# The factor on the probabilities as a constant 67th row of the score product, and a 66-column transposition of the maxima

## The chip, the core and the metric

The kernel runs on one core of one Trainium2 chip. The metric is the device time of one execution in microseconds (us), as a median over runs. Five engines work side by side, each with a queue of its own: TensorE (PE; its weight loads are shown apart as PEld), VectorE (DVE), ScalarE (ACT), GpSimd (POOL) and SyncE (SP), which here issues the DMA transfers.

## What is computed

One encoder layer is applied to 2048 and to 512 tokens of width 1024: normalisation, one projection, attention beside a two-way gated linear attention, an output projection, an embedding gate and a last normalisation. The change lies in the attention. There are 8 query heads and 2 key heads of width 64:

```python
s = jnp.einsum('bkgqd,btkd->bkgqt', q_blk, k).astype(jnp.float32) * scale
p = jax.nn.softmax(s, axis=-1)
return jnp.einsum('bkgqt,btkd->bkgqd', p.astype(v.dtype), v)
```

## The kernel before

Stage 1 projects and rotates, stage 2 builds the linear attention, stage 3 is the attention with the gates, stage 4 the output. Stage 3 works through 40 items: a block of 512 queries of one head. The first four blocks have 2048 keys (16 key tiles of 128), the fifth has 512 (4 tiles), so there are 32 x 16 + 8 x 4 = 544 key tiles in all.

Queries and keys are split into a high and a low half of 16 bits. Two products of 512 columns (L861, L862) put the transposed scores of one key tile into PSUM (`pss`): `qa` and `ka` hold 128 rows, `qb` and `kb` hold 64 rows of q's high half and k's low half, and two rows more. In these rows `kb` has the constant 4096 (L747, written by POOL) and `qb` has minus the query's maximum over 4096, as a 16-bit value and its rest. So the score comes out with the maximum already taken off. ScalarE then makes the probability `p` (L863): exp(qk_scale * pss + ln 256), where the scale `qk_scale` and the bias `lnp` are both a column of one value for each partition. It rounds `p` to 16 bits (`phi`, L870), two key tiles at a time; VectorE takes the rest (`plo`, L872); TensorE multiplies both by the values (`po`, L842 and L850) and by ones (`pz`, L846). L842 and L846 use 32 columns of weights at a time, at four places of the array, the other products 128.

The maxima are computed some heads' tiles ahead (function `maxima`): products `px` (L807), a reduction of each by VectorE (`mx`, L813), one over the tiles (L817), and two instructions that write `mt`, 128 x 4 blocks x 2 (L821, L822). Four products (L825) with the 2 columns of a block of `mt` as weights and the identity as the moving operand, 128 columns wide, turn it into two rows of 512 in a `px` buffer of PSUM. ScalarE copies the two rows to partitions 64 and 65 of `qb` (L826).

The order on each queue is set as follows. `stage3` walks over the items; in `head`, after each Exp, `pull` takes steps from generators: the maxima of later items (`mg`, with counts in `steps`), the rest of stage 2 (`fin`), the gates (`gt`, L773), the sums and the stores. `tc.issue_after(e.ins)` puts what a step issues on ScalarE behind that Exp. Buffers are reused in turn: 4 for `qa` and for `qb`, 3 for `mt`, `p` and the small tiles, 2 and then 3 of PSUM for `pss`, 2 for `px`. `load_q` issues the two loads of an item from SP (L755, L756) when its maxima begin.

Of the kernel before, what the change touches and what calls it, by code (L numbers as in the profile page):

```python
# [9 lines left out]
F32 = mybir.dt.float32  # L10
F32R = mybir.dt.float32r
F16 = mybir.dt.float16
BF16 = mybir.dt.bfloat16
U32 = mybir.dt.uint32
AF = mybir.ActivationFunctionType
ALU = mybir.AluOpType
# [4 lines left out]
P = 128  # L21
# [3 lines left out]
P_SCALE = 256.0  # L25
V_LIMIT = 1024.0
QK_SCALE = 1024.0
M_SCALE = 4096.0
# [27 lines left out]
class Net:  # L56
    def __init__(self, tc, d, ctx):
        self.tc, self.nc, self.d = tc, tc.nc, d
        nc = self.nc
        nc.scalar.preload_act_table_set("natural_log_exp_and_others")  # L60
        self.cp = ctx.enter_context(tc.tile_pool(name="cp", bufs=1))
        self.sm = ctx.enter_context(tc.tile_pool(name="sm", bufs=3))
        self.ident = self.cp.tile([P, P], F32, name="ident")
        make_identity(nc, self.ident)
        self.identh = self.cp.tile([P, P], F16, name="identh")
        nc.vector.tensor_copy(self.identh, self.ident)
        self.lnp = self.cp.tile([P, 1], F32, name="lnp")
        nc.vector.memset(self.lnp, math.log(P_SCALE))
        self.qk_scale = self.cp.tile([P, 1], F32, name="qk_scale")
        self.mhalf = self.cp.tile([P, 1], F32, name="mhalf")  # L70
        nc.vector.memset(self.mhalf, -0.5)
        self.half = self.cp.tile([P, 1], F32, name="half")
        nc.vector.memset(self.half, 0.5)
        self.one = self.cp.tile([P, 1], F32, name="one")
        nc.vector.memset(self.one, 1.0)
        self.plen = self.cp.tile([P, 8], F32, name="plen")
        self.vinv = self.cp.tile([P, 2], F32, name="vinv")

        self.wdiv = self.cp.tile([P, 3], F32, name="wdiv")
# [38 lines left out]
def stage1(net, s, gw):  # L118
    nc, tc, d = net.nc, net.tc, net.d
    with ExitStack() as ctx:  # L120
# [223 lines left out]
        nc.scalar.activation(qa, qn, AF.Abs)  # L344
        big = net.sm.tile([P, 2], F32, name="big")
        nc.vector.tensor_reduce(big, qa, axis=AX.X, op=ALU.max)
        nc.vector.tensor_scalar(big, big, 1e-18, None, ALU.max)
        inv = net.sm.tile([P, 2], F32, name="inv")
        nc.vector.reciprocal(inv, big)
        for w in range(2):  # L350
# [363 lines left out]
def stage3(net, s, fin=iter(()), top=None, tail=None):  # L714
    nc, tc, d = net.nc, net.tc, net.d
    with ExitStack() as ctx:
# [3 lines left out]
        cp = pool("s3c", 1)  # L720
# [3 lines left out]
        qp = pool("s3q", 4)  # L724
# [10 lines left out]
        ones = cp.tile([P, 32], F16, name="ones")  # L735
        nc.vector.memset(ones, 1.0)

        def load_k(c):
            kp = kl[c]
            ka = kp.tile([P, 2, 512], F16, name="ka")  # L740
            kb = kp.tile([P, 2, 512], F16, name="kb")
            v = kp.tile([P, 4, 2, P], F16, name="v")
            src = s["kt"][c].rearrange("l (k d) t -> l d k t", k=2)
            for j in range(2):
                nc.sync.dma_start(out=ka[j * 64:(j + 1) * 64], in_=src[0])
            nc.sync.dma_start(out=kb[0:64], in_=src[1])
            nc.gpsimd.memset(kb[64:66], M_SCALE)  # L747
            nc.sync.dma_start(out=v, in_=s["vs"][c].rearrange("t p k e -> p t k e"))
            return ka, kb, v

        def load_q(c, h):
            src = s["qt"][c][:, h // 2, (h % 2) * 64:(h % 2) * 64 + 64]
            qa = qp.tile([P, 512], F16, name="qa")
            qb = qp.tile([P, 512], F16, name="qb3")
            nc.sync.dma_start(out=qa, in_=src)  # L755
            nc.sync.dma_start(out=qb[0:64], in_=src[0])  # L756
            return qa, qb
# [43 lines left out]
        def maxima(idx, c, h, q):  # L801
            ks = keys(c)
            n = len(ks)
            mx = net.sm.tile([P, 4, n], F32, name=f"mx{n}")
            def product(ti, b):
                ps = ps_x.tile([P, 512], F32, name="px", tag="px")
                nc.tensor.matmul(ps, lhsT=q[0][:, b * P:(b + 1) * P], rhs=ks[ti][0][:, h // 4],  # L807
                                 start=True, stop=True)
                return ps

            for b in range(4):
                for i in range(n):
                    nc.vector.tensor_reduce(mx[:, b, i:i + 1], product(i, b), axis=AX.X, op=ALU.max)  # L813
                    yield
            if n > 1:
                m = net.sm.tile([P, 4], F32, name="m")
                nc.vector.tensor_reduce(m, mx, axis=AX.X, op=ALU.max)  # L817
            else:
                m = mx[:, :, 0]
            mt = net.sm.tile([P, 4, 2], F16, name="mt")  # L820
            nc.vector.tensor_scalar(mt[:, :, 0], m, -1.0 / M_SCALE, None, ALU.mult)  # L821
            nc.vector.scalar_tensor_tensor(mt[:, :, 1], m, -1.0 / M_SCALE, mt[:, :, 0], ALU.mult, ALU.subtract)  # L822
            ps = ps_n_tile()
            for b in range(4):
                nc.tensor.matmul(ps[0:2, b * P:(b + 1) * P], lhsT=mt[:, b], rhs=net.identh, start=True, stop=True)  # L825
            nc.scalar.copy(q[1][64:66], ps[0:2])  # L826

        def head(ks, h, q, ou, pull, last):
            kv = h // 4
# [24 lines left out]
            for t in range(0, n, 2):  # L854
                p = pp.tile([P, 2, 512], F32, name="p", bufs=3)
                for i in range(2):
                    ka, kb = ks[t // 4][:2]
                    cs = slice((t % 4 + i) * P, (t % 4 + i + 1) * P)
                    ps = ps_s[0].tile([P, 512], F32, name="pss")
                    ps_s.append(ps_s.pop(0))  # L860
                    nc.tensor.matmul(ps, lhsT=ka[:, kv, cs], rhs=q[0], start=True, stop=False)  # L861
                    nc.tensor.matmul(ps, lhsT=kb[0:66, kv, cs], rhs=q[1][0:66], start=False, stop=True)  # L862
                    e = nc.scalar.activation(p[:, i], ps, AF.Exp, bias=net.lnp, scale=net.qk_scale)  # L863
                    with tc.issue_after(e.ins):
                        pull(t + i, n)
                hi = pp.tile([P, 2, 512], F16, name="phi", bufs=4)
                if last and t % 8 == 6:
                    nc.vector.tensor_copy(hi, p)
                else:
                    nc.scalar.copy(hi, p)  # L870
                lo = pp.tile([P, 2, 512], F16, name="plo", bufs=4)
                nc.vector.tensor_tensor(lo, p, hi, ALU.subtract)  # L872
                pend.append((t, hi, lo))
                if len(pend) == 3:
                    pv([pend.pop(0) for _ in range(2)])
# [41 lines left out]
        kset, gs, qs = {}, {}, {}  # L917
# [8 lines left out]

        def all_maxima():
            for i, (c, h) in enumerate(items):
                qs[i] = load_q(c, h)
                yield from maxima(i, c, h, qs[i])  # L930
                yield

# [316 lines left out]
```

## Time and profile before

| | us |
|---|---|
| median of 3 runs (2069.65 to 2073.27) | 2069.95 |
| the profiled execution, its own time | 2074.57 |
| its span, first to last instruction | 2072.9 |
| granted TensorE clock over the span | 0.981 of 2.4 GHz |

The page of the profile gives for each engine its busy time, then the span in 40 slices, the DMA queues, the chain of work that ended last, and the costliest groups of instructions. A group's row reads: line, engine, operation, output <- inputs, shapes, count | busy us, mean ns of one | idle time of the engine before it, and who ended it. Matmuls are pipelined, so the start of one to the start of the next is what it costs, not its duration.

### The profile page before, as it was taken

The page shows a single profiled execution, that of the slowest core. Times are in us where ns is not written, and L with a number is a line of the kernel's source. Part 1 is how long each engine was busy: PE and PEld are TensorE (multiplying, and loading weights), DVE is VectorE, ACT ScalarE, POOL GpSimd, SP SyncE. Part 2 cuts the span into 40 slices and gives each one's busy share as a digit, 9 for nine tenths or more (in the row PEclk, how much of TensorE's full clock was granted, in tenths as well). Part 3 has the DMA queues.
Part 4 walks back from the last instruction along what each step waited for, and adds up shares of the span by engine and source line. Part 5 has one row for each costly group of instructions (what it writes and reads, how often), then busy time and mean ns, then how long its engine had stood idle before and what let it go on. Part 6 is the DMA issues. An engine that isn't in the chain of part 4 may idle for free.

```text
span 2072.9 us, 29975 instructions
## 1 busy us (share of the span) xinstructions
PE 1963.8 (95%) x11096; PEld 1224.5 (59%) x11096; DVE 1318.6 (64%) x2272; ACT 1220.7 (59%) x2136; POOL 350.1 (17%) x293
## 2 busy tenths in 40 slices
PE   8999998999879999999999999999978999999998
PEld 6888886555654433433333343343346888888886
DVE  7557755666668889889889988988863222222223
ACT  6645443555548889889889888878863222222222
POOL 2444441000331001011011100101011111111111
PEclk9999999999989999999999999999989999999999
DMA  7745945454666113322223322312235222222220
GB/s 236 223 116 132 225 105 140 119 160 146 208 207 213 61 62 121 95 88 84 82 89 108 111 69 71 110 53 68 83 110 153 86 87 87 87 87 87 82 67 33
DMA packets 264226, 235.79 MB, mean 114 GB/s; under 512 B 107312, under 2 KB 199312, under 8 KB 264080
## 3 DMA queue, kind: packets, MB, share of 16 engines
q1 hardware_dynamic: 263936, 233.36, 37.8%
q8 instruction: 87, 1.43, 0.3%
q14 instruction: 59, 0.48, 0.1%
q0 software_dynamic: 144, 0.52, 0.1%
HBM read 157.46 MB, written 76.37 MB: 113 GB/s over the span
## 4 chain that ended last, share of the span: by engine, by line
PE 69%; DVE 12%; ACT 9%; DMA 5%; issue 3%; POOL 1%; SPq 0%; DVEq 0%; POOLq 0%; ACTq 0%
PE pm L114 38%; PE pg L773 6%; PE po L850 4%; ACT p L863 4%; DVE plo L872 4%; PE px L807 4%; DVE mx L813 3%; PE pss L862 3%; PE pss L861 3%; ACT phi L870 3%; PE pp L114 3%; PE po L842 2%; PE pz L846 2%; DMA scr_ga<-a 1%; DMA qa<-scr_qt 1%
## 5 line engine op out<-in xcount | busy, mean ns | idle before, releaser
L863 ACT ACTIVATE p<-pss,lnp,qk_scale 128x512 f32<-128x512 f32 x544 | 408.0, 781 | 94.6 <-PE pss L862 90.8
L813 DVE TENSOR_REDUCE mx<-px 128x1 f32<-128x512 f32 x544 | 358.8, 683 | 74.2 <-PE px L807 71.7
L872 DVE TENSOR_TENSOR plo<-p,phi 128x1024 f16<-128x1024 f32 x272 | 344.4, 1266 | 37.4 <-ACT phi L870 34.2
L870 ACT CAST phi<-p 128x1024 f16<-128x1024 f32 x270 | 282.9, 1048 | 4.5
L773 PE MATMUL pg<-xt,wg 128*128 128x512 f16 x960 | 277.3, 378 | 0.5
L807 PE MATMUL px<-ka,qa 128*128 128x512 f16 x544 | 199.8, 382 | 20.0 <-DVE mx L813 11.7
L861 PE MATMUL pss<-qa,ka 128*128 128x512 f16 x544 | 206.8, 381 | 10.1 <-ACT p L863 9.3
L862 PE MATMUL pss<-qb,kb 66*128 66x512 f16 x544 | 208.1, 383 | 0.0
L773 PEld LDWEIGHTS <-wg 128*128 128x128 f16 x960 | 92.8, 97 | 119.2 <-issue 10.1
L1182 DVE SCALAR_TENSOR_TENSOR th<-th,pp 128x512 f32<-128x512 f32 (+1 forms) x41 | 27.7, 675 | 190.6 <-ACT th L1181 190.6
L850 PE MATMUL po<-phi,v 128*128 128x512 f16 x544 | 142.2, 384 | 0.0
L1135 ACT CAST hT<-pt 128x512 fp32r<-128x512 f32 x40 | 23.5, 587 | 166.9 <-PE pt L1134 166.9
L114 PE MATMUL pm<-xt,whl 128*128 128x512 f16 x480 | 108.5, 386 | 2.4 <-ACT l L494 2.4
L114 PE MATMUL pm<-wq_h,xt 128*128 128x512 f32 x320 | 104.2, 406 | 4.6 <-ACT xt L239 4.1
L114 PE MATMUL pm<-wo1h,mx 128*128 128x512 f32 x320 | 102.7, 403 | 5.3 <-ACT wo1h L1083 5.3
L1181 ACT ACTIVATE th<-pm,rh 128x512 f32<-128x512 f32 (+1 forms) x41 | 27.8, 679 | 134.7 <-PE pm L114 134.7
L903 POOL TENSOR_TENSOR ou<-ou,rs 128x512 f32<-128x512 f32 x20 | 32.8, 1639 | 435.3 <-DMA rs<-scr_rc 367.6
L114 PE MATMUL pm<-wpg0h,hT 128*128 128x512 f32 x320 | 101.8, 398 | 4.4 <-ACT hT L1135 4.2
L114 PE MATMUL pm<-wo0h,mx 128*128 128x512 f32 x320 | 101.0, 396 | 0.0
L862 PEld LDWEIGHTS <-kb 66*128 66x128 f16 x544 | 53.0, 97 | 79.9 <-issue 22.8
L114 PE MATMUL pm<-wpg1h,hT 128*128 128x512 f32 (+1 forms) x336 | 99.6, 379 | 0.0
L114 PE MATMUL pm<-wl_h,xt 128*128 128x512 f32 x320 | 99.6, 392 | 0.0
(267 smaller groups left out, 3785.0 us busy)
## 6 DMA issues: line engine op xcount, KB each, us to landing
wg<-scr_wg SPq DMA_DIRECT2D x40, 512.0 KB
scr_mx<-hl SPq DMA_DIRECT2D x40, 512.0 KB
mx<-scr_mx SPq DMA_DIRECT2D x20, 1024.0 KB
x<-x_prompt SPq DMA_DIRECT2D x27, 512.0 KB
scr_xt<-xh SPq DMA_DIRECT2D x20, 512.0 KB
xt<-scr_xt SPq DMA_DIRECT2D x20, 512.0 KB
xt<-scr_xt SPq DMA_DIRECT2D x40, 256.0 KB
wstage<-w_in SPq DMA_DIRECT2D x32, 256.0 KB
```

The lines of the kernel that those rows point to most:

```text
L114: self.nc.tensor.matmul(out, lhsT=a[k], rhs=b[k], start=first and i == 0, stop=last and i == n - 1)
L773: nc.tensor.matmul(ps, lhsT=w[:, wi, k], rhs=xi, start=i == 0, stop=i == 23)
L807: nc.tensor.matmul(ps, lhsT=q[0][:, b * P:(b + 1) * P], rhs=ks[ti][0][:, h // 4], start=True, stop=True)
L813: nc.vector.tensor_reduce(mx[:, b, i:i + 1], product(i, b), axis=AX.X, op=ALU.max)
L842: nc.tensor.matmul(po[r:r + 32], lhsT=ks[t // 4][2][:, t % 4 + i, kv, g * 32:g * 32 + 32], rhs=lo[:, i], start=t == 2, stop=False)
L846: nc.tensor.matmul(pz[i * 32:i * 32 + 32], lhsT=ones, rhs=(lo, hi)[i // 2][:, i % 2], start=t == 2, stop=t + 4 == n)
L850: e = nc.tensor.matmul(po, lhsT=ks[t // 4][2][:, t % 4 + i, kv], rhs=hi[:, i], start=False, stop=t + i + 1 == n)
L861: nc.tensor.matmul(ps, lhsT=ka[:, kv, cs], rhs=q[0], start=True, stop=False)
L862: nc.tensor.matmul(ps, lhsT=kb[0:66, kv, cs], rhs=q[1][0:66], start=False, stop=True)
L863: e = nc.scalar.activation(p[:, i], ps, AF.Exp, bias=net.lnp, scale=net.qk_scale)
L870: nc.scalar.copy(hi, p)
L872: nc.vector.tensor_tensor(lo, p, hi, ALU.subtract)
```

## The change

The factor 256 on the probabilities is no longer added as the bias of the Exp. It becomes one more row of the product L862: `kb` has 4096 in row 66 as well, and `qb` has ln(256) / (4096 * qk_scale) there, which does not change from item to item. For that the four buffers of `qb` become tiles of their own, written once at the start of stage 3 (rows 64 to 66, of which L826 overwrites two). The transposition of the maxima uses 66 columns of weights, of which the first 64 are zero and written once, in three tiles of their own; its two rows of interest come out at partitions 64 and 65. A lower bound in stage 1 (for the division by qk_scale) becomes 0.5.

```diff
-        self.lnp = self.cp.tile([P, 1], F32, name="lnp")
-        nc.vector.memset(self.lnp, math.log(P_SCALE))
...
-        nc.vector.tensor_scalar(big, big, 1e-18, None, ALU.max)
+        nc.vector.tensor_scalar(big, big, 0.5, None, ALU.max)
...
+        lnp = cp.tile([P, 1], F32, name="lnp")
+        nc.vector.reciprocal(lnp, net.qk_scale)
+        nc.vector.tensor_scalar(lnp, lnp, math.log(P_SCALE) / M_SCALE, None, ALU.mult)
+        qbs = [cp.tile([P, 512], F16, name=f"qb{i}") for i in range(4)]
+        for qb in qbs:
+            nc.vector.tensor_copy(qb[64:67], lnp[64:67].broadcast_to([3, 512]))
+        mts = [cp.tile([P, 4, 66], F16, name=f"mt{i}") for i in range(3)]
+        for mt in mts:
+            nc.gpsimd.memset(mt, 0.0)
...
-            nc.gpsimd.memset(kb[64:66], M_SCALE)
+            nc.gpsimd.memset(kb[64:67], M_SCALE)
...
-            qb = qp.tile([P, 512], F16, name="qb3")
+            qb = qbs[idx % 4]
...
-            mt = net.sm.tile([P, 4, 2], F16, name="mt")
-            nc.vector.tensor_scalar(mt[:, :, 0], m, -1.0 / M_SCALE, None, ALU.mult)
-            nc.vector.scalar_tensor_tensor(mt[:, :, 1], m, -1.0 / M_SCALE, mt[:, :, 0], ALU.mult, ALU.subtract)
+            mt = mts[idx % 3]
+            nc.vector.tensor_scalar(mt[:, :, 64], m, -1.0 / M_SCALE, None, ALU.mult)
+            nc.vector.scalar_tensor_tensor(mt[:, :, 65], m, -1.0 / M_SCALE, mt[:, :, 64], ALU.mult, ALU.subtract)
             ps = ps_n_tile()
             for b in range(4):
-                nc.tensor.matmul(ps[0:2, b * P:(b + 1) * P], lhsT=mt[:, b], rhs=net.identh, start=True, stop=True)
-            nc.scalar.copy(q[1][64:66], ps[0:2])
+                nc.tensor.matmul(ps[0:66, b * P:(b + 1) * P], lhsT=mt[:, b], rhs=net.identh, start=True, stop=True)
+            nc.scalar.copy(q[1][64:66], ps[64:66])
...
-                    nc.tensor.matmul(ps, lhsT=kb[0:66, kv, cs], rhs=q[1][0:66], start=False, stop=True)
-                    e = nc.scalar.activation(p[:, i], ps, AF.Exp, bias=net.lnp, scale=net.qk_scale)
+                    nc.tensor.matmul(ps, lhsT=kb[0:67, kv, cs], rhs=q[1][0:67], start=False, stop=True)
+                    e = nc.scalar.activation(p[:, i], ps, AF.Exp, scale=net.qk_scale)
```

## Rows read from the trace of the kernel before

**Rows 1.** Page, part 1: busy us of each engine.
```profile
PE 1963.8 (95%) x11096; PEld 1224.5 (59%) x11096; DVE 1318.6 (64%) x2272; ACT 1220.7 (59%) x2136; POOL 350.1 (17%) x293
```
**Rows 2.** Busy time by stretch: stretch, its length, then each engine, clock, DMA.
```profile
565.00:1500.00 935.00, 886.82 (x5638) 381.31 (x5637) 797.48 (x1145) 775.60 (x1117) 118.24 (x82) 0.99 0.31 99
1500.00:1525.00 25.00, 19.78 (x121) 6.98 (x117) 18.14 (x22) 23.51 (x35) 0.00 (x0) 0.85 0.41 127
```
**Rows 3.** Waits of PE, 565 to 1525 us: total us, times, longest.
```profile
PE px L807 <- DVE mx L813: 11.7, 18, 2.9
PE pss L861 <- ACT p L863: 9.3, 13, 1.8
PE po L842 <- DVE plo L872: 9.1, 23, 1.6
PE pn L825 <- DVE mt L822: 8.8, 12, 1.3
```
**Rows 4.** Waits of DVE, 565 to 1525 us.
```profile
DVE mx L813 <- PE px L807: 71.7, 119, 3.6
DVE plo L872 <- ACT phi L870: 34.2, 65, 2.1
```
**Rows 5.** Groups of ACT, shapes apart.
```profile
L863 ACT ACTIVATE p<-pss,lnp,qk_scale 128x512 f32<-128x512 f32 x544 | 408.0, 781 | 94.6 <-PE pss L862 90.8 <-DVE rsum L895 1.5
...
L777 ACT ACTIVATE g<-pg,gdiv 128x512 f32<-128x512 f32 x40 | 27.2, 681 | 0.0
...
L495 ACT ACTIVATE l<-l 128x512 f32<-128x512 f32 x20 | 12.7, 633 | 0.3
```
**Rows 6.** ACT in order of time: start, us, instruction (two Exps in a row).
```profile
1103.47 1.45 ACT L863 ACTIVATE p<-pss,lnp,qk_scale 128x512 f32<-128x512 f32 x2
```
**Rows 7.** ACT in order of time, behind the last head.
```profile
1529.68 3.18 ACT L105 ACTIVATE wpg0h<-wstage,plen 128x512 fp32r<-128x512 f32 x5
...
1542.21 3.22 ACT L1083 CAST wo1h<-wo1raw 128x512 fp32r<-128x512 f32 x6
```
**Rows 8.** PE in order of time around one transposition of the maxima.
```profile
1126.78 1.04 PE L850 MATMUL po<-phi,v 128*128 128x512 f16 x4
1127.74 0.38 PE L825 MATMUL pn<-identh,mt 128*2 128x128 f16 x4
1128.06 0.39 PE L807 MATMUL px<-ka,qa 128*128 128x512 f16 x1
```
**Rows 9.** Groups of PE and of its weight loads (PEld), shapes apart.
```profile
L825 PE MATMUL pn<-identh,mt 128*2 128x128 f16 x160 | 15.4, 218 | 9.1 <-DVE mt L822 8.8
...
L862 PEld LDWEIGHTS <-kb 66*128 66x128 f16 x544 | 53.0, 97 | 79.9 <-issue 22.8
...
L825 PEld LDWEIGHTS <-mt 128*2 128x2 f16 x160 | 7.9, 82 | 27.1 <-DVE mt L822 22.4 <-issue 3.8 <-DVE plo L872 0.8
```
**Rows 10.** The chain that ended last, 600 to 1500 us, shares of that stretch.
```profile
by line: PE pg L773 14.2%; PE po L850 8.7%; DVE plo L872 8.4%; ACT p L863 8.2%; PE px L807 7.8%; DVE mx L813 6.9%; PE pss L862 6.4%; PE pss L861 6.2%; ACT phi L870 5.7%; PE po L842 5.2%; issue 4.6%; PE pz L846 3.9%; DMA qa<-scr_qt 1.6%; DMA
```
**Rows 11.** The same chain, 1500 to 1525 us (the last head).
```profile
by line: ACT p L863 24.2%; ACT phi L870 20.2%; PE po L850 11.2%; issue 7.7%; ACT wo0h L1030 7.4%; PE po L842 6.3%; PE pz L846 5.1%; DVE plo L872 4.9%; PE pss L861 3.5%; ACT ou L881 2.7%; PE pss L862 2.6%; ACT hl L794 2.0%; ACT acc L878 1.9%
```
**Rows 12.** DVE in order of time at the start of stage 3.
```profile
566.08 0.09 DVE L736 MEMSET ones<- 128x32 f16 x1
568.05 0.17 DVE L84 TENSOR_SCALAR o_ms<-os 128x4 f32<-128x4 f32 x1 [1.89 <-ACT osq L618]
569.41 0.69 DVE L671 TENSOR_TENSOR on<-pf,o_r 128x512 f32<-128x512 f32 x1 [1.19 <-POOL o_r L86]
573.70 0.69 DVE L813 TENSOR_REDUCE mx<-px 128x1 f32<-128x512 f32 x1 [3.60 <-PE px L807]
```
**Rows 13.** Groups of DVE, shapes apart.
```profile
L813 DVE TENSOR_REDUCE mx<-px 128x1 f32<-128x512 f32 x544 | 358.8, 683 | 74.2 <-PE px L807 71.7
...
L895 DVE RECIPROCAL rsum<-rsum 32x32 f32<-32x32 f32 x20 | 6.7, 335 | 0.2
```
**Rows 14.** The DMA queue of SP in order of time, start of stage 3.
```profile
565.74 0.61 SPq L755 DMA_DIRECT2D qa<-scr_qt  x1
...
566.87 0.54 SPq L756 DMA_DIRECT2D qb<-scr_qt  x1
```

More of the change, by code (lines that the diff above doesn't have):

```diff
@@ L746, in load_k, with load_q @@
             nc.sync.dma_start(out=kb[0:64], in_=src[1])
-            nc.gpsimd.memset(kb[64:66], M_SCALE)
+            nc.gpsimd.memset(kb[64:67], M_SCALE)
             nc.sync.dma_start(out=v, in_=s["vs"][c].rearrange("t p k e -> p t k e"))
             return ka, kb, v
-        def load_q(c, h):
+        def load_q(idx, c, h):
             src = s["qt"][c][:, h // 2, (h % 2) * 64:(h % 2) * 64 + 64]
             qa = qp.tile([P, 512], F16, name="qa")
-            qb = qp.tile([P, 512], F16, name="qb3")
+            qb = qbs[idx % 4]
             nc.sync.dma_start(out=qa, in_=src)
@@ L928, in all_maxima @@
             for i, (c, h) in enumerate(items):
-                qs[i] = load_q(c, h)
+                qs[i] = load_q(i, c, h)
                 yield from maxima(i, c, h, qs[i])
```

## The prediction

> **What bounds the kernel now.** I read the profile from the whole to the part. The page's first part shows TensorE busy for 95% of the span, with ScalarE and VectorE near 60% [rows 1]; that is an average over four stages, and the change lies in one of them. So the next view is busy time by stretch. In stage 3, from 565 to 1500 us, TensorE is busy 886.8 of 935 us, VectorE 797.5 and ScalarE 775.6 [rows 2]: three engines at 95, 85 and 83%, which feed each other through few buffers. In the last 25 us, when nothing but the last head is left, ScalarE is the fullest, 23.5 of 25 [rows 2].
>
> The waits of TensorE tell who stops it: the reductions of the maxima 11.7 us, the Exp (which frees the PSUM of the scores) 9.3 us, `plo` 9.1 us and `mt` 8.8 us in 12 waits [rows 3]. VectorE in turn waits 71.7 us for TensorE's products and 34.2 us for ScalarE's `phi` [rows 4]. So `plo` is partly late because ScalarE is. No engine stands alone: the limit passes from one to the next, mostly TensorE.
>
> **The change, part by part.**
>
> *The Exp loses its bias column.* The Exp reads two columns, `lnp` and `qk_scale`, and takes 781 ns; an activation of the same shape from PSUM with one column (L777) takes 681; an Exp without any, from SBUF, 633 [rows 5]. So a column costs about 100 ns, and a bias that isn't given shows no operand and no cost. Does that hold when instructions follow one another? Two Exps in a row take 1.45 us, a step of 1.45 - 0.78 = 0.67 [rows 6]. Five activations in a row with one column take 3.18 us, 0.64 each, and six without 3.22, 0.54 each [rows 7]. In a row too it is 0.1 us for each column. ScalarE is thus freed of 544 x 0.1 = 54 us.
>
> What is that worth? ScalarE isn't the bound: its Exps wait 90.8 us for scores [rows 5]. I read it from the chain that ended last. In the 900 us from 600 to 1500 the Exp holds 8.2%, 73.8 us [rows 10]; in the last head 24.2% of 25 us, 6.1 us [rows 11]. At 0.67 to 0.68 us each, (73.8 + 6.1)/0.68 = 117 Exps of 544 lie on it. All of them shorter give 117 x 0.1 = 11.7 us, and that is the ceiling as long as the order of the queues stays; the floor is nothing. I take two thirds, 7.8 us, since the other engines stand close behind: where the Exp no longer ends a wait, VectorE's `plo` or `mx` is late next, from its 85%.
>
> *The transposition uses 66 columns.* Around one transposition, the four products of L850 start 0.22 us apart ((1.04 - 0.38)/3), the last at 1127.44; the first of L825 starts at 1127.74, 0.30 later; its four start 0.05 apart ((0.38 - 0.22)/3), the last at 1127.90; the next product starts at 1128.06, 0.16 later [rows 8, 9]. So to go from 128 columns of weights to few costs about 0.09 us over the usual step, and to go back about 0.10. No row has 66 columns beside 128, so between nothing and all of it may go; 66 is more than half of 128, and I take both as gone: 40 ways out at 0.10 make 4.0 us, and 40 - 12 = 28 ways in at 0.09 make 2.5 us, since in 12 of them TensorE waits for `mt` anyway [rows 3]. That is 6.5 us of TensorE's time. Its lines hold 52% of the chain and the sequencer's "issue" 5% more [rows 10], so I take two thirds again, 4.3 us; the ceiling is 6.5, the floor nothing. (The Trainium skill, "TensorEngine Tiling (Array Packing)", sections on tiling modes and key properties, has column tiles of 32, 64 or 128 and says that a change of mode drains the engine; by it 66 columns run in the mode of the products around them, and no run here shows that yet.)
>
> The cost against it is the load of 66 columns of weights instead of 2. Loads of 2 and of 128 columns last 82 and 97 ns [rows 9], so 66 last something between, and the question is whether they hide behind products that start 0.05 us apart. Nothing in the trace shows 66 columns. Bounds: no cost if hidden; if each of the 160 loads stands free, at 0.10 us, 16 us more. I take none, as the loads of 2 columns last 82 ns and hide behind these same steps. The Trainium skill, "TensorE: Matmul & The Clock Gate", section on weight-path perf modes, speaks against this: the fast load of weights is used only for 128 columns; its section on LDWEIGHTS gives columns / 1.2 as the ns of a load, so by an estimate from that page 55 ns for 66 columns, just the step of these products, and the sum would stay as it is or grow by a few us.
>
> *The rest costs nothing that I can find.* A 67th row in L862 adds neither column nor product. `kb`'s memset has three partitions for two, the same columns. The copy to `qb` reads two partitions as before. `mt` is written with a longer stride, four elements a partition. No DMA is added; `qb`'s load waits for the reader four items back, as before, and `mt` for the one three back. The new work stands at the start of stage 3: on VectorE a reciprocal (0.34 us), a multiplication (0.17) and four fills of 512 columns (0.34 to 0.68 each, between the two rows nearest) [rows 12, 13], 1.9 to 3.2 us together. They stand behind the memset of `ones` and ahead of L84 (for which POOL and then L671 wait); VectorE idles there 1.89 + 1.19 + 3.60 = 6.7 us before the first reduction at 573.70 [rows 12], because the products wait for the load of `qa`. That idle time hides them. If the fills must come before the load of `qb`, issued at 566.87 right behind that of `qa` [rows 14], SP holds the following key loads for as long. Without cover it is 3 us at most. Three small memsets go to POOL, which is busy 17% of the time [rows 1]. The changed lower bound is a constant in one instruction.
>
> **The sum.** 2074.57 us of the profiled execution, less 7.8, less 4.3, makes 2062.5. That execution stands 4.6 above the median of the runs shown (2069.95); against the median the sum is 2057.9, so 2058.
>
> **The rivals.** About 0.2%, or 4.1 us, is what a measurement of this kernel can tell from no change; so faster begins below 2065.8 and slower above 2074.1.
>
> 1. *More than the chain shows.* `plo` waits for `phi`, and the reductions stand behind `plo` on VectorE, so a faster ScalarE can take away part of every wait in rows 3 but that for `mt`. The ceilings alone give 11.7 + 6.5 = 18.2, 2051.8. If all waits for Exp and `plo` went (18.4) with the 6.5, it is 24.9, 2045. For it: 34.2 us of VectorE's waiting for ScalarE [rows 4]. Against it: VectorE at 85% remains.
>
> 2. *ScalarE's time is hidden, or isn't freed.* If the 54 us fall into the Exp's own 90.8 us of waiting, only TensorE's part stays: 4.3 to 6.5, so 2063.5 to 2065.7. It comes out the same if a missing bias is read as a column of zeros and the Exp stays at 781; the 633 of L495 speaks against that [rows 5].
>
> 3. *Slower: the loads of 66 columns stand in TensorE's way.* Place: the four products of L825. Price: each load not hidden costs up to 0.10 us, 160 of them 16 us, on the engine with 95%; against 7.6 us that the ways in and out cost now over all 40. From a step of about 0.10 us instead of 0.05 on, the transposition loses. With the full price, ScalarE's part hidden and two thirds of it on the chain, (16 - 6.5) x 2/3 = 6.3 more: 2076. For it: no row shows such a load hidden. Against: 82 ns are hidden now.
>
> **How the numbers follow.** The forecast, with its own range of 2053 to 2063, gets 0.52. Rival 1 gets 0.18, rival 2 gets 0.18, rival 3 gets 0.08, and 0.04 is left for the queues' order coming out otherwise, to either side. Faster: 0.52 + 0.18 + half of rival 2, and a little of the last, 0.80. Same: the other half of rival 2 and some of rival 3 in milder form, 0.12. Slower: 0.08. The range for 8 in 10 reaches over most of rivals 1 and 2: 2047 to 2067.
>
> **What would show it.** Right: the Exp's group at about 680 ns; L825 to the next product 0.05 instead of 0.16, and the start of its first 0.22 behind the product before; the ScalarE total down by some 54 us; TensorE's waits for Exp and `plo` smaller, stage 3 shorter by about 12 us, stages 1, 2 and 4 as they were. Wrong: an Exp at 781; a step within L825 near 0.1; waits for `mx` or `mt` that grow by what the others lose; products at the start of stage 3 later than 573 us behind the fills.

## The result and the profile after

The changed kernel takes 2054.26 us (median of 4 runs, 2054.19 to 2054.36), the kernel before 2071.38 (4 runs); the ratio is 0.9918, 95% interval 0.9902 to 0.9934. The forecast was 2058.0, with a range of 2047 to 2067. So time and sign came out as told, 4 us further down than the sum. The profiled execution went from 2074.57 to 2054.25, 20.3 us. That is more than the 12.1 of the sum, and the parts of it aren't those of the sum, as the experiments show.

**What came as foretold.** Page, part 1, of the kernel after:

```profile
PE 1952.0 (95%) x11096; PEld 1220.6 (59%) x11096; DVE 1316.1 (64%) x2277; ACT 1177.7 (57%) x2136; POOL 352.7 (17%) x296
```

ScalarE's total fell by 43.0 us against [rows 1], not by 54. The Exp's group and the activation it was compared with, in the groups of ACT with shapes apart:

```profile
L874 ACT ACTIVATE p<-pss,qk_scale 128x512 f32<-128x512 f32 x544 | 361.4, 691 | 122.7 <-PE pss L873 118.7 <-DVE m L828 1.5
...
L788 ACT ACTIVATE g<-pg,gdiv 128x512 f32<-128x512 f32 x40 | 27.3, 682 | 0.0
```

781 became 691 ns [rows 5], 0.09 us for the column that is gone. The group holds 46.6 us less, and its idle time grew from 94.6 to 122.7 us: ScalarE spends more than half of what it was given waiting for scores.

The transposition, PE in order of time (start, us, instruction), and its groups on PE and PEld:

```profile
947.81 1.04 PE L861 MATMUL po<-phi,v 128*128 128x512 f16 x4
948.68 0.39 PE L836 MATMUL pn<-identh,mt 128*66 128x128 f16 x4
948.91 0.38 PE L818 MATMUL px<-ka,qa 128*128 128x512 f16 x1
```
```profile
L836 PE MATMUL pn<-identh,mt 128*66 128x128 f16 x160 | 16.2, 223 | 9.6 <-DVE mt L833 9.5
L836 PEld LDWEIGHTS <-mt 128*66 128x66 f16 x160 | 11.1, 110 | 24.6 <-DVE mt L833 20.0 <-issue 2.2
```

From the first of the four products of L861 to the product behind the transposition it is 948.91 - 947.81 = 1.10 us, where [rows 8] have 1128.06 - 1126.78 = 1.28. Here both ways are gone: the first of the four starts 0.21 behind the product ahead of it (948.68, less 947.81 + 1.04 - 0.38), and the next stands (948.91 - 948.68) = 0.23 behind the first, of which the four's own steps take 0.17 and the way out 0.05 to 0.06.

Over all 40 transpositions it is less even. The way out fell from 0.152 to 0.056 us in all but one. The way in was 0.31 in the 23 that didn't wait before; now it is 0.22 in 15 and 0.27 to 0.31 in ten, and the rest wait. In 24 of the 40 the second product starts 0.08 us behind the first instead of 0.055, so there the load of 66 columns isn't wholly hidden. That is about 39 x 0.096 + 15 x 0.093 + 7 x 0.04 less 24 x 0.025, or about 5 us saved at the place, of the 6.5 of the ceiling.

TensorE's waits, 565 to 1525 us (total us, times, longest), against [rows 3]:

```profile
PE px L818 <- DVE mx L824: 10.5, 15, 2.9
PE pn L836 <- DVE mt L833: 9.5, 13, 1.3
PE pss L872 <- ACT p L874: 9.0, 17, 1.5
PE po L853 <- DVE plo L883: 5.2, 11, 1.5
PE px L818 <- DMA qa<-scr_qt: 3.0, 1, 3.0
```

`plo` fell from 9.1 to 5.2, `mx` from 11.7 to 10.5. The wait for the Exp stayed at 9.0, and that for `mt` rose from 8.8 to 9.5. Such sums don't repeat well, though: in a second profile of the same changed kernel (`c1_after`, below) the wait for `plo` is

```profile
PE po L853 <- DVE plo L883: 8.1, 13, 1.5
```

against 8.9 in the second profile of the kernel before, so the fall of `plo` isn't shown. The chain that ended last, 600 to 1500 us, by line, against [rows 10]:

```profile
by line: PE pg L784 14.6%; PE po L861 10.2%; PE px L818 8.2%; DVE plo L883 7.9%; PE pss L873 7.6%; PE pss L872 7.4%; ACT p L874 6.4%; PE po L853 5.9%; ACT phi L881 5.5%; DVE mx L824 5.2%; issue 4.7%; PE pz L857 4.6%; DMA qa<-scr_qt 1.4%; PE
```

Here the gain can be seen: the Exp holds 6.4% of 900 us, 57.6, instead of 73.8, and TensorE's `po` and `pss` have taken its place. This view repeats better: in the second pair of profiles (below) the Exp's share falls from 8.9% to 7.1%, by 1.8 points as here.

**What wasn't foreseen.** The new constants lie in the pool in front of all of stage 3's later buffers, so these moved up by 1536 bytes in each partition. By the addresses that the program gives its pools, the `xt` buffers of the gates no longer meet the last buffers of stage 2, and the gates' own pool, which ended below stage 4's first buffers, now reaches into them. Two groups of transfers stand elsewhere in SP's queue: the eight loads of `xt` for the first gates are issued in stage 2 (352 to 365 us instead of 631 to 638), and four loads of the embedding gate's weights, which stood ahead at 1489.95 us, are issued with the rest behind the heads (1531.49). To see what each part does I cut every profile at four points: the start of the first `px`, of the first Exp and of the last Exp, and the end. The stretch from first to last Exp is the cleanest measure of the heads' work, since neither stage 2 nor the wait for the first loads is in it.

| profile | first px | first to last Exp | last Exp to end |
|---|---|---|---|
| before | 573.1 | 911.2 | 549.4 |
| after | 563.3 | 902.8 | 545.1 |

So there are three parts: 9.7 us ahead of the heads, 8.4 in them, 4.3 behind them (and 2.0 given back between first `px` and first Exp, 41.3 us instead of 39.3, where TensorE waits 3.0 us for a load of `qa`). In the second pair of profiles, `c0_before` and `c1_after` below, the same parts are 3.5, 6.9 and 4.4 us. The forecast had all of it in the second.

### The profile page after: what moved, and what is told of

It reads as the page before. It is cut to its first block, busy times and chain, and to the rows that moved or that the text cites. A ratio compares the mean times of both kernels' runs of the same rounds, so it can differ in the third digit from the quotient of the medians.

```text
span 2052.5 us, 29960 instructions
## 1 busy us (share of the span) xinstructions
PE 1952.0 (95%) x11096; PEld 1220.6 (59%) x11096; DVE 1316.1 (64%) x2277; ACT 1177.7 (57%) x2136; POOL 352.7 (17%) x296
## 4 chain that ended last, share of the span: by engine, by line
PE 50%; DVE 8%; ACT 7%; DMA 3%; issue 2%; POOL 1%; SPq 0%; POOLq 0%; DVEq 0%; ACTq 0%
PE pm L112 20%; PE pg L784 6%; PE po L861 5%; PE px L818 4%; DVE plo L883 4%; PE pss L873 3%; PE pss L872 3%; ACT p L874 3%; PE po L853 3%; PE pp L112 2%; ACT phi L881 2%; DVE mx L824 2%; PE pz L857 2%; PE pt L1145 1%; DMA qa<-scr_qt 1%
## 5 line engine op out<-in xcount | busy, mean ns | idle before, releaser
L874 ACT ACTIVATE p<-pss,qk_scale 128x512 f32<-128x512 f32 x544 | 361.4, 691 | 122.7 <-PE pss L873 118.7
L883 DVE TENSOR_TENSOR plo<-p,phi 128x1024 f16<-128x1024 f32 x272 | 339.3, 1248 | 36.2 <-ACT phi L881 34.2
L818 PE MATMUL px<-ka,qa 128*128 128x512 f16 x544 | 199.7, 382 | 19.8 <-DVE mx L824 10.5
L873 PE MATMUL pss<-qb,kb 67*128 67x512 f16 x544 | 207.5, 383 | 0.0
L861 PE MATMUL po<-phi,v 128*128 128x512 f16 x544 | 142.7, 385 | 0.0
L873 PEld LDWEIGHTS <-kb 67*128 67x128 f16 x544 | 53.0, 97 | 78.1 <-issue 22.4
```

The source lines that it names most:

```text
L861: e = nc.tensor.matmul(po, lhsT=ks[t // 4][2][:, t % 4 + i, kv], rhs=hi[:, i], start=False, stop=t + i + 1 == n)
L873: nc.tensor.matmul(ps, lhsT=kb[0:67, kv, cs], rhs=q[1][0:67], start=False, stop=True)
L874: e = nc.scalar.activation(p[:, i], ps, AF.Exp, scale=net.qk_scale)
```

## The experiments

Each ratio is to the runs of the kernel before on the same chip. `e1` to `e4` ran on one chip, `c0`, `c1`, `e5` and `e6` on a second, `e7` to `e9` on a third, so rows are compared across chips by their ratios alone. The last three columns are from one profiled execution each.

| run | bias | 66 columns | bytes moved | ratio (interval) | first px | first to last Exp | to end |
|---|---|---|---|---|---|---|---|
| c0_before | | | 0 | 1.0003 (0.9990 to 1.0017) | 568.6 | 911.4 | 549.3 |
| e1_bias_only | yes | | 0 | 0.9977 (0.9966 to 0.9988) | 568.6 | 905.0 | 550.3 |
| e2_cols66_only | | yes | 992 | 0.9982 (0.9970 to 0.9993) | 570.6 | 912.3 | 545.3 |
| e3_both_two_mt | yes | yes | 992 | 0.9943 (0.9927 to 0.9959) | 567.6 | 905.3 | 544.4 |
| e4_pad_only | | | 1536 | 0.9968 (0.9957 to 0.9980) | 567.7 | 910.8 | 544.4 |
| e5_pad_992 | | | 992 | 0.9977 (0.9967 to 0.9987) | 567.9 | 914.9 | 543.5 |
| e6_bias_pad_992 | yes | | 992 | 0.9942 (0.9927 to 0.9957) | 566.2 | 905.5 | 544.9 |
| e7_gate_pad | | | 992, gates | 0.9983 (0.9970 to 0.9996) | 572.0 | 914.5 | 545.4 |
| c1_after | yes | yes | 1536 | 0.9935 (0.9918 to 0.9952) | 565.1 | 904.4 | 545.0 |
| e8_after_narrow | yes | 2 of 66 | 1536 | 0.9938 (0.9923 to 0.9953) | 563.7 | 904.2 | 545.5 |
| e9_no_columns | yes, no scale | yes | 1536 | 0.9913 (0.9901 to 0.9925) | 566.4 | 900.0 | 545.9 |

Two things stand out over all thirteen profiles (these eleven, and the first two of the kernel before and of the changed one). From first to last Exp the six kernels' profiles that keep the bias take 910.8 to 914.9 us, and the seven without it 905.5 or less. From the last Exp to the end the three that leave the gates' pool where it was take 549.3 to 550.3 us, and the other ten 543.5 to 545.9. Each of the two gains shows wherever its cause is present.

**The two kernels again.** The kernel before and the changed one, unchanged, as others were profiled.

> The kernel before, unchanged, profiled once more. If the 4 to 5 us by which all four runs so far were ahead of the first profile at stage 3's first product (568 to 571 against 573 us) are only that execution's own slowness, the first product is near 569 here and the span near 2069. If the placement of buffers makes them, it is near 573 again.

Median 2071.93. The first `px` starts at 568.6, not 573.1: 4.5 of the 9.7 us ahead of the heads are a difference between two executions of the same kernel. The heads (911.4) and the end (549.3) repeat within 0.2 us of the profile before.

> The changed kernel, unchanged, beside the other kernels on one chip. Theory A (both edits and the stage-4 transition that the shifted buffers shorten): 12 to 13 us below before, like the run with two mt tiles. Theory B (the early xt loads add to that in stage 2): 16 to 18 us below before, with the first product of stage 3 at about 563 us and 4 us below the run with two mt tiles.

Median 2057.16 (6 runs, 2054.73 to 2063.62). The 2054.26 of the first four runs lies below all six; the gain is 13.5 us by this ratio and 17.0 by the first. The result stands between the two theories, and the first `px` (565.1) too. The heads took 904.4 us, 1.6 more than in the first profile of this kernel.

**The bias alone.** The whole change but for the transposition: `mt`, L825 and L826 as before.

```diff
+            nc.vector.tensor_copy(qb[64:67], lnp[64:67].broadcast_to([3, 512]))
...
-                    nc.tensor.matmul(ps, lhsT=kb[0:66, kv, cs], rhs=q[1][0:66], start=False, stop=True)
-                    e = nc.scalar.activation(p[:, i], ps, AF.Exp, bias=net.lnp, scale=net.qk_scale)
+                    nc.tensor.matmul(ps, lhsT=kb[0:67, kv, cs], rhs=q[1][0:67], start=False, stop=True)
+                    e = nc.scalar.activation(p[:, i], ps, AF.Exp, scale=net.qk_scale)
```

> The kernel before with the factor as 67th row and no bias, but the 2-column transposition; the buffers behind the constants stay where they were (stage 3's xt buffers still begin at 138528). Theory A (the chain's Exps and the transposition make the gain, all in stage 3): about 8 to 11.7 us below before. Theory B (half of the gain comes from the eight xt loads that the shifted buffers let go early, in stage 2): 5 us or less of the stage-2 time changes, first px product near 573 us as before, and only some 4 to 7 us in all. In both the Exp is at 691 ns.

Median 2066.70; 0.0023 of 2071.4 is 4.8 us (2.5 to 7.0). The buffers behind the heads' own lie as before, the end is 1 us later than before (550.3), and the heads' stretch is shorter by 911.35 - 905.02 = 6.3 us than in `c0_before`. So the gain lies in the heads, where the prediction put it. Its size falls short of the first theory; it is that of the second, whose early loads are put to the test below.

**The transposition alone**, with two `mt` tiles instead of three, which moves the buffers by 992 bytes.

```diff
+        mts = [cp.tile([P, 4, 66], F16, name=f"mt{i}") for i in range(2)]
...
-                nc.tensor.matmul(ps[0:2, b * P:(b + 1) * P], lhsT=mt[:, b], rhs=net.identh, start=True, stop=True)
-            nc.scalar.copy(q[1][64:66], ps[0:2])
+                nc.tensor.matmul(ps[0:66, b * P:(b + 1) * P], lhsT=mt[:, b], rhs=net.identh, start=True, stop=True)
+            nc.scalar.copy(q[1][64:66], ps[64:66])
```

> The kernel before with the 66-column transposition alone (two mt tiles instead of three, so that the xt buffers of stage 3 still share memory with stage 2's last u tile), bias kept. Theory A: 4 to 6.5 us below before. Theory B: 1 to 4 us. In both the product after the last of the four follows 0.055 us later instead of 0.152.

Median 2067.12, 3.7 us less (0.0018), which by itself looks like the forecast's 4.3. The cut says otherwise: the heads took 912.3 us, no less than before, and the gain stands behind them, 545.3 instead of 549.3. Both theories allow the size, and this run can't tell the columns from the bytes.

**Both, with two `mt` tiles.** The changed kernel with `range(2)` and `idx % 2`.

> The changed kernel with two mt tiles instead of three, which puts the xt buffers of stage 3 back onto memory that stage 2 still uses (139520 instead of 140064), so that their loads can't go early. Theory A: within 1 us of the changed kernel. Theory B: 5 to 10 us above the changed kernel, the first px product near 573 us again.

Median 2058.79, 4.5 us above the first median of the changed kernel and 1.6 above the second. Neither theory holds: it isn't within 1 us of the first, and the first `px` stands at 567.6, not near 573. Heads 905.3, end 544.4. Against the transposition alone, which has the same bytes, the bias is worth 0.9982 - 0.9943 = 0.0039, 8.1 us, and 7.0 in the heads.

**Bytes alone.** The kernel before with an unused tile in the pool of the constants, and nothing else: 1536 bytes a partition as in the changed kernel.

```diff
         nc.vector.memset(ones, 1.0)
+        cp.tile([P, 768], F16, name="pad")
```

> The kernel before with nothing but 1536 unused bytes a partition among stage 3's constants: the xt buffers begin at 140064, as in the changed kernel, and their eight first loads are issued in stage 2. Theory A: within 1 us of before. Theory B: 6 to 10 us below before, the first px product near 564 us, and the time between the first and the last Exp as before.

Median 2064.78, 6.6 us less (4.1 to 8.9) for a tile that nobody uses. Its heads took 910.8 us, as before; its end 544.4. The size is that of the second theory, but not the place: the first `px` stands at 567.7, not near 564, within 1 us of the control, and the gain lies behind the heads, where neither theory had it. The same with 992 bytes, to stand beside the transposition alone:

```diff
+        cp.tile([P, 496], F16, name="pad")
```

> The kernel before with 992 unused bytes a partition among stage 3's constants: stage 3's later buffers shift as in the run with two mt tiles, but the xt buffers still meet stage 2's last u tile, so no load goes early in stage 2. If the stage-3 to stage-4 transition alone is what the shift changes: 4 to 5 us below before, all of it after the last Exp. If the shift does nothing by itself: within 1 us of before.

Median 2066.55, 4.8 us less by the ratio, as expected. Behind the last Exp it is 5.8 us less than in the control, but the heads took 914.9 us, 3.6 more, for no added work; why is open. The bytes without the transposition gain 1.0 us more than with it, so they are enough to account for that run's 3.7. In the heads alone the transposition's run is 2.6 us the shorter.

**The bias with the bytes**, `e1_bias_only` with the 992-byte tile, so that it stands beside both with two `mt` tiles.

> The bias removed and the 67th row in use, 2-column transposition, with the same shift of 992 bytes. Theory A: the bias is worth 4.7 us (as measured alone) and the shift 4 to 5 us more, so 9 to 10 us below before, and the two add up. If the shift gave nothing of its own: 4 to 5 us below before.

Median 2058.78, and 2058.79 with the 66 columns on top. The heads are 905.5 and 905.3. Against the same bytes alone the bias is worth 0.9977 - 0.9942 = 0.0035, 7.3 us, and 914.9 - 905.5 = 9.4 in the heads. The two together give 0.0058, 12.0 us, more than the 9 to 10 expected and than the 9.6 of the two runs apart.

**Where the bytes act.** The unused tile now lies in the pool of the gates alone, behind everything that the heads use.

```diff
                 gp = pool("s3g", 2)
+                gp.tile([P, 496], F16, name="pad", bufs=1)
```

> The kernel before with 992 unused bytes per partition in the gates' own pool alone, so that this pool ends later and so do the buffers behind it that the gates load and compute with, while everything that the attention heads of stage 3 use stays where it was; the arithmetic is as before. If the gain of the pads comes from where stage 4's first buffers (trp) meet the gates' pool, and so from the order of the queues between stages 3 and 4 (the four w_ple_gate loads issued with the others, the first hT split ahead of the wpp splits), then the stretch from the last Exp to the end is 544 to 546 us as with the pads (549 to 550 before), the stretch of the heads is as before (950 to 954), and the time is 4 to 6.5 us under before. If the gain comes from the heads' buffers lying elsewhere, or the pads' gain was only the programs' spread, it is within 2 us of before, with 549 to 550 us behind the last Exp.

Median 2067.72, 3.5 us less by the ratio (0.8 to 6.2), a little short of the expected 4 to 6.5. The profiled execution was a late one (first `px` at 572.0), and its heads took 3.2 us more than the control's (914.5, open as above), but behind the last Exp it took 545.4 us, as in every kernel that moved the gates' pool. So that pool's place is enough for the gain behind the heads. The queues show how. SP of the control in order of time, then of this run:

```profile
1485.60 2.01 SPq L103 DMA_DIRECT2D wstage<-w_ple_gate  x4
...
1544.15 10.39 SPq L103 DMA_DIRECT2D wstage<-w_ple_gate  x11
1554.89 2.21 SPq L103 DMA_DIRECT2D wstage<-w_ple_proj  x3
```
```profile
1549.87 12.80 SPq L103 DMA_DIRECT2D wstage<-w_ple_gate  x15
```

VectorE of the control, where the last Exp starts at 1519.21, and of this run, where it starts at 1526.12:

```profile
1559.25 1.29 DVE L106 SCALAR_TENSOR_TENSOR wpp0l<-wstage,wpp0h 128x512 fp32r<-128x512 f32 x2
1561.83 0.69 DVE L106 SCALAR_TENSOR_TENSOR wpp1l<-wstage,wpp1h 128x512 fp32r<-128x512 f32 x1 [1.29 <-ACT wpp1h L105]
1562.44 0.42 DVE L1136 TENSOR_TENSOR pT<-pt,pT 128x256 fp32r<-128x256 f32 x1
1562.77 0.68 DVE L1136 TENSOR_TENSOR hT<-pt,hT 128x512 fp32r<-128x512 f32 x1
```
```profile
1564.16 0.68 DVE L1137 TENSOR_TENSOR hT<-pt,hT 128x512 fp32r<-128x512 f32 x1
1565.41 2.74 DVE L106 SCALAR_TENSOR_TENSOR wpg1l<-wstage,plen,wpg1h 128x512 fp32r<-128x512 f32 x4 [0.57 <-ACT wpg1h L105]
1568.07 0.69 DVE L106 SCALAR_TENSOR_TENSOR wpp0l<-wstage,wpp0h 128x512 fp32r<-128x512 f32 x1
```

In the control the first `hT` of stage 4 (the input of the embedding gate's products) stands on VectorE behind three splits of `wpp`, one of which waits for ScalarE and that for a transfer: 1562.77 - 1519.21 = 43.6 us after the last Exp. With the bytes moved the four loads no longer go ahead, the order of what follows comes out otherwise, and `hT` stands ahead of those splits: 1564.16 - 1526.12 = 38.0. All thirteen profiles agree: the first `hT` starts 43.6 to 45.4 us after the last Exp, with three of the four splits of `wpp` ahead of it, where the gates' pool lies as before, and 37.2 to 39.3 after it, with none ahead, in the other ten. TensorE can begin the gate's products while the rest of the weights is still on its way. Busy time by stretch (stretch, length, then PE, PEld, DVE, ACT, POOL, granted clock, DMA share, GB/s), 30 to 60 us behind the last Exp, control and this run:

```profile
1549.20:1559.20 10.00, 4.89 (x23) 3.34 (x21) 8.11 (x13) 8.05 (x15) 0.00 (x0) 0.94 0.79 256
1559.20:1569.20 10.00, 7.88 (x21) 5.62 (x22) 4.56 (x10) 2.40 (x5) 0.57 (x1) 0.55 1.08 308
1569.20:1579.20 10.00, 10.00 (x47) 8.26 (x46) 0.69 (x1) 1.71 (x4) 1.28 (x1) 1.00 0.07 21
```
```profile
1556.10:1566.10 10.00, 5.99 (x28) 4.57 (x27) 8.38 (x17) 9.11 (x16) 0.57 (x1) 0.95 0.83 273
1566.10:1576.10 10.00, 8.81 (x34) 6.67 (x33) 5.41 (x10) 3.82 (x7) 0.00 (x0) 0.88 1.00 298
1576.10:1586.10 10.00, 10.00 (x46) 8.20 (x45) 2.22 (x6) 3.67 (x9) 2.72 (x3) 1.00 0.38 102
```

In the first two rows (20 us) TensorE had 44 products at work in the control and 62 here, and its granted clock in the second 10 us was 0.55 of full speed, near the lower of its two levels (1.2 GHz of 2.4), against 0.88; in the 10 us ahead it had been busy for 4.9 us there and 6.0 here. Once all weights are there both run at 1.00.

**What 66 columns are worth.** The changed kernel with its buffers where they are, but the weights of each product of the transposition are only columns 64 and 65, and only rows 64 and 65 are written. The zeros left out are read by nobody.

```diff
-                nc.tensor.matmul(ps[0:66, b * P:(b + 1) * P], lhsT=mt[:, b], rhs=net.identh, start=True, stop=True)
+                nc.tensor.matmul(ps[64:66, b * P:(b + 1) * P], lhsT=mt[:, b, 64:66], rhs=net.identh, start=True, stop=True)
```

> The changed kernel with its buffers where they are, but each product of the transposition takes only the two columns of mt that hold the maxima as weights (64 and 65) and writes only rows 64 and 65; the rows that are left out are zeros that nobody reads. Prediction's term for the 66 columns: 40 ways out and 28 ways in come back, 4.3 us slower than the changed kernel (ceiling 6.5). Theory from the runs so far: the saved time comes back as waits for mt and plo, so within 2 us of the changed kernel, though the product behind each transposition starts 0.15 us later again instead of 0.055. Rival that 66 columns stand in the way: faster than the changed kernel.

PE in order of time at the place shown above for the kernel after:

```profile
947.87 1.04 PE L861 MATMUL po<-phi,v 128*128 128x512 f16 x4
948.84 0.38 PE L836 MATMUL pn<-identh,mt 128*2 128x128 f16 x4
949.16 0.39 PE L818 MATMUL px<-ka,qa 128*128 128x512 f16 x1
```

1.29 us again instead of 1.10: the two ways are back, 0.19 us. Yet the ratio is 0.9938 (2059.24 us) beside 0.9935 for the changed kernel, 0.6 us apart with intervals of 3 us to each side, and the heads took 904.2 us beside 904.4 and 902.8. So most of TensorE's time that was saved at that place wasn't time of the kernel. The intervals leave room for 2 or 3 us, and the ratio of the changed kernel's first four runs (0.9918) would make 4.1 of it; the three pairs that differ in the columns alone (this one, `e3` against `e6`, `e2` against `e5`) give by their ratios 0.6 less, 0.2 more and 1.0 more for the 66 columns. Against the unused tile of the same 1536 bytes (`e4_pad_only`) this run also gives the bias by itself once more: 0.9968 - 0.9938 = 0.0030, 6.2 us, and 6.6 in the heads.

**How much of ScalarE's time still counts.** The changed kernel with the scale written into the Exp as a number, the one that these inputs give, instead of the column that the program computes from them. The Exp then reads no column.

```diff
-                    e = nc.scalar.activation(p[:, i], ps, AF.Exp, scale=net.qk_scale)
+                    e = nc.scalar.activation(p[:, i], ps, AF.Exp, scale=9.49071693588481e-06)
```

> The changed kernel with the scale of the Exp written into the instruction as a number (for these inputs) instead of read from a column that the program computes; so the Exp reads no column at all. It should fall from 691 to about 590 to 600 ns, 544 x 0.1 = 54 us less of ScalarE. Theory that ScalarE's time on the path of the heads is still worth what it was for the bias (4.5 to 9 us for 0.1 us an Exp): 2046 to 2053, the stretch from the first px to the last Exp at 936 to 940 us. Rival, that with the bias gone the Exp is behind TensorE and VectorE and further time on it is hidden: within 2 us of the changed kernel, that stretch at 942 to 945, and TensorE's waits for p smaller but those for mx and mt larger.

Its Exp group on ACT, and TensorE's waits from 565 to 1525 us:

```profile
L874 ACT ACTIVATE p<-pss 128x512 f32<-128x512 f32 x544 | 313.2, 600 | 159.4 <-PE pss L873 154.7 <-DVE mt L832 1.6
```
```profile
PE px L818 <- DVE mx L824: 10.9, 17, 2.9
PE po L853 <- DVE plo L883: 9.5, 17, 1.3
PE pn L836 <- DVE mt L833: 8.5, 11, 2.2
PE px L818 <- DMA qa<-scr_qt: 6.5, 2, 4.7
PE pss L872 <- ACT p L874: 5.3, 10, 1.4
```

600 ns, and the heads took 900.0 us, 2.8 and 4.5 less than in the two profiles of the changed kernel. From first `px` to last Exp it is 939.5, within the expected 936 to 940; the median of 2053.24 is just past the 2053. So ScalarE's time seems still to count, at a lower price: the wait for the Exp fell to 5.3, and `plo`, VectorE's work, stands at 9.5 (5.2 and 8.1 in the two profiles of the changed kernel). By the ratios it is 0.0022, 4.6 us, below the changed kernel, but the two intervals overlap (0.9901 to 0.9925 and 0.9918 to 0.9952), so it isn't shown by the times. It has the lowest ratio of all, yet it is no replacement as it stands, since the number holds for these inputs.

## Why the prediction was right, and where it was not

- **The Exp's bias: right.** 0.1 us an Exp was 0.09 (691 ns), and two thirds of the chain's 11.7 us, 7.8, measured 4.8, 7.3, 8.1 and 6.2 us by the ratios of four pairs (`e1`, `e6` to `e5`, `e3` to `e2`, `e8` to `e4`) and 6.3, 9.4, 7.0 and 6.6 in the heads. The place was right too. The chain was the right view for it, its Exps fell from 73.8 to 57.6 us. The waits were not: "TensorE's waits for Exp and `plo` smaller" did not hold for the Exp (9.3 to 9.0 and 9.6 in two profiles, with 17 and 18 times for 13 [rows 3]) and isn't shown for `plo` (9.1 to 5.2 and 8.1). Rival 1 in its full form, in which all of these waits go, falls with that. Its 2051.8 from the two ceilings is nearer to the first median than the forecast, but not for its reason: the columns gave far less than their ceiling, and part of the gain lies behind the heads.
- **The total of ScalarE, 54 us less: 43.0.** The Exps' group gave 46.6. Rival 2, in which the freed time is hidden or the Exp stays at 781 ns, falls by `e1_bias_only`, where the bias alone is 2.5 to 7.0 us; `e9_no_columns` makes it likely that even the next 0.09 us isn't wholly hidden.
- **The transposition: this is the term that was mis-sized.** "I take two thirds again, 4.3 us" measured about nothing (0.6 us less to 1.0 more by the ratios of three pairs; 2.6 less to 0.2 more in the heads of the same pairs). The steps before it held in the main: both ways went, 0.18 to 0.19 us at the place shown, and about 5 of the 6.5 us over all 40. What failed is the reading from TensorE's 52% of the chain to two thirds of what is saved at one place. The transposition stands between two waits for VectorE, for `mt` ahead of it and `plo` and `mx` behind it; TensorE that comes sooner finds them no sooner. Between 565 and 1525 us its waits for `mt` and `mx` are 9.5 and 10.5 us with 66 columns (10.5 and 11.0 in the second profile), 8.4 and 9.8 with two; in 604 to 1508 us it was busy 867.2 and 870.3 of 904 us in the two profiles of the changed kernel and 872.1 with the narrow weights. So the saving appears as idle time. That it goes into these two waits is an argument, not shown: of the other pairs one agrees (20.2 and 18.8 us for `mt` and `mx` together, `e3` and `e6`) and one doesn't (19.6 and 20.5, `e2` and `e5`).
- **Rival 3, loads of 66 columns that stand in the way: refuted but for a small rest.** They last 110 ns, outside the 82 to 97 that the prediction took as bounds [rows 9], and most of them hide: 95 of 119 steps between the four products are 0.055 to 0.059 us, as before. The other 24, each the first of its transposition, are 0.08, which makes 24 x 0.025 = 0.6 us against the 16 of the full price. The transposition as a whole got cheaper: the way out costs 0.10 us with 2 columns and nothing with 66, the way in 0.09 with 2, and with 66 nothing in 15 cases and some 0.05 to 0.10 in ten. The estimate of 55 ns from the Trainium skill ("TensorE: Matmul & The Clock Gate", section on LDWEIGHTS) is half of the 110 measured. The same page of the Trainium skill, section on weight-path perf modes, has the fast load on for 128 columns; that a load of 66 lasts longer than one of 128 (97 ns) fits it. The Trainium skill, "TensorEngine Tiling (Array Packing)", sections on tiling modes and key properties, by which 66 columns run in the mode of the products around them, agrees with the two ways' going where they went.
- **"The rest costs nothing that I can find": right for the instructions, wrong for the buffers.** The fills are hidden, as told. VectorE in order of time at the start of stage 3, after, beside [rows 12]:

```profile
557.22 0.13 DVE L738 RECIPROCAL lnp<-qk_scale 128x1 f32<-128x1 f32 x1
557.38 0.15 DVE L739 TENSOR_SCALAR lnp<-lnp 128x1 f32<-128x1 f32 x1
557.57 1.42 DVE L742 CAST qb<-lnp 3x512 f16<-3x512 f32 x4
559.19 0.17 DVE L82 TENSOR_SCALAR o_ms<-os 128x4 f32<-128x4 f32 x1 [0.20 <-ACT osq L616]
560.49 0.69 DVE L669 TENSOR_TENSOR on<-pf,o_r 128x512 f32<-128x512 f32 x1 [1.13 <-POOL o_r L84]
563.77 0.69 DVE L824 TENSOR_REDUCE mx<-px 128x1 f32<-128x512 f32 x1 [2.59 <-PE px L818]
```

They take 1.7 us, a little less than the 1.9 to 3.2 foretold, and the idle time around them went from 6.7 to 3.9. The 67th row is free as told: the product takes 383 ns with 66 rows (L862) and with 67 (L873). But the prediction counted instructions and not bytes. "Stages 1, 2 and 4 as they were" failed: 3 to 7 us of the gain lie behind the last Exp (549.3 to 550.3 us, against 543.5 to 545.9) and come from where buffers lie. Nor is stage 3 shorter by the 12 us foretold: from first to last Exp it is 8.4 and 6.9 in the two pairs of profiles.

**The sum by its parts.** By the ratios, moved buffers give 3.5 to 6.6 us, the bias 4.8 to 8.1 and the columns about 0; that is 8 to 15, where 13.5 and 17.0 were measured for the whole. On the changed kernel's own layout the steps are 6.6 for the bytes (`e4`), 6.2 for the bias (`e8`) and 0.6 for the columns (`c1`). Two errors of the sum, some 4 too much for the columns and 3.5 to 6.6 left out, nearly cancelled; that the forecast's time came out so near is in part luck.

**What stays open.** The 3.5 us between the two measurements of the changed kernel, whose intervals overlap (0.9902 to 0.9934 and 0.9918 to 0.9952); the 2.4 us by which the bias and 992 bytes together gave more than apart; and the 3 to 4 us by which moved bytes alone lengthened the heads in two runs (`e5`, `e7`). In the four profiles of kernels on the changed layout with all its parts the first `px` starts at 563.3 to 566.4 us, in the other nine at 566.2 to 573.1. The early loads of `xt` fall there, but `e4_pad_only` has them and starts at 567.7, and the same kernel varies by 4.5 us in this place. It isn't shown that they help.

## What to carry to other kernels

Time that an engine saves at one place is worth something only if the next thing it waits for comes sooner too: the same two thirds of a ceiling were right for the Exp, whose result others waited for, and wrong for the transposition, which stood between two waits for another engine. A change that adds or moves buffers should be timed against a control with the same bytes and no work: here an unused tile gave 3.5 to 6.6 us mostly by the order in which transfers and queues came out behind the heads. And one profile of each kernel isn't enough to say where time went; cut several at the same landmarks.

## What the runs showed of the hardware

An operand that is a column costs an Exp of 128x512 from PSUM 90 ns each: 781, 691 and 600 ns with two, one and none (the kernel before, after, `e9_no_columns`). A product of 512 columns takes 383 ns with 66 or 67 rows. A load of 66 columns of weights lasts longer (110 ns) than one of 128 (97) or of 2 (82), and still hides behind most products that start 0.055 us apart: only 24 of 119 steps grew, to 0.08. In the narrow version (`e8_after_narrow`) a load of 2 columns behind products with 128 starts late; PEld in order of time, narrow and then after:

```profile
1115.93 0.55 PEld L861 LDWEIGHTS <-v 128*128 128x128 f16 x4 [0.42 <-issue]
1116.90 0.08 PEld L836 LDWEIGHTS <-mt 128*2 128x2 f16 x1 [0.42 <-issue]
```
```profile
1115.41 0.55 PEld L861 LDWEIGHTS <-v 128*128 128x128 f16 x4 [0.42 <-issue]
1116.08 0.38 PEld L836 LDWEIGHTS <-mt 128*66 128x66 f16 x3
```

Two columns wait 0.42 us behind the last load of `v`, 66 columns follow it in 0.12 (1116.08 - 1115.41 - 0.55). The first product of the transposition comes 0.10 us sooner there (0.21 instead of 0.31 behind the last of L861): at this place 66 columns were loaded ahead and 2 were not.
